# Opening the gate of the late output stores half a store earlier, in a batched matmul on one core

## The chip, the core and the metric

The kernel runs on one core of a Trainium2 chip. The metric is device microseconds of that core; the profile's span, from the first to the last instruction, is some 1.8 us shorter (515.2 beside 516.97 for the changed kernel). The executions of most kernels here lie within 0.3% of each other (six of the kernel before: 516.89 to 517.77 us), those of gate498, gate500, k8, pool8a and pool8b within 0.4 to 0.6%. All executions quoted here are marked as fast in their records. Every timed run was made in rounds with the kernel before on the same chip, and the ratio is formed from those rounds.

Names used below: TensorE (PE) does the matmuls, VectorE (DVE) and ScalarE (ACT) copy results out of PSUM (the memory that TensorE writes to), GpSimd (POOL) and SyncE (SP) issue DMAs. The data itself is moved by DMA engines, of which the profile counts 16. In the profile, q0 is the queue that POOL issues to, q1 the one that SP issues to, and q8 is of the kind "instruction": its packets follow the number of TensorE's instructions (20 for 5218, 15 for 3874, 8 for 2082, under A1 and mm5 below). The queues get in each other's way: from 495 to 500 us in the trace before, q1 takes 68.2% of the 16 engines' time, q0 24.8% and q8 1.2%, 94% in all, and in gate29, below, stores on q1 stretch the last loads of weights on q0 from 27.5 to 38.8 us (issue to landing).

## The reference

```python
x      = randn(32, 512, 1024)    # float32: batch, m, k
weight = randn(32, 1024, 768)    # float32: batch, k, n
out    = matmul(x, weight)       # float32: 32, 512, 768
```

## The kernel before

Loads go through q0, all but that of the first x, and are cast to bf16 on the way (the page: 167.77 MB read from HBM, but 126.88 MB moved on q0, of which 44.04 are the 28 stores). For each of 32 batches TensorE transposes x, multiplies, and the two copying engines empty PSUM into an output tile. A batch's output is one 1.5 MB tile: row tiles 0 and 1 are its first column half ("pair 0" below), row tiles 2 and 3 its second. The stores of batches 0 to 27 go through q0, between the loads. The stores of 28 to 31 are "late": they go through SP's queue.

SP issues the stores in the program's order, and it needs something to hold 28 and 29 back, whose data is ready long before (that of 29 at 477.64; in the trace before both go out behind the store of 30, the three within 3.20 us from 495.14). This is the gate: the store of 30, placed first. Its wait for the data of 30 (493.9 us from the start, below) delays everything behind it.

```python
    CHUNKED = {B - 4: (4, 4), B - 3: (4, 4), B - 2: (4, 4), B - 1: (4, 2, 2)}
    AHEAD = 3
    LATE = 4
    # ... pools, views ...
        for b in range(B):
            # ... load x of b + 4 and weights of b + 3, on gpsimd ...
            if 0 < b <= B - LATE:
                nc.gpsimd.dma_start(out=out_view[b - 1], in_=outs[b - 1])
            if b == B - 1:
                for late in (B - 2, *range(B - LATE, B - 2)):
                    nc.sync.dma_start(out_view[late], outs[late])
            outs[b] = out_pool.tile([P, MT * N], F32, name="out_sb")
            # ... batches that are not CHUNKED: two pairs of row tiles over all of k ...
            xT = {0: transpose(b, 0)}
            pms = [banks() for _ in range(2)]
            at = 0
            for n in CHUNKED[b]:
                last = at + n == KT
                for mt in range(MT):
                    if mt + 1 not in xT and mt + 1 < MT:
                        xT[mt + 1] = transpose(b, mt + 1)
                    matmuls(pms[mt // 2], mt % 2, xT[mt], b, range(at, at + n), True)
                    if last and mt % 2 == 1:
                        pair = mt // 2
                        evacuate(b, pair, pms[pair])
                        if b == B - 1:
                            cols = slice(pair * N2, (pair + 1) * N2)
                            nc.sync.dma_start(out_view[b, :, cols], outs[b][:, cols])
                at += n
```

## Time and profile before

| | before |
|---|---|
| median of 3 runs | 517.37 us (517.19 to 517.54) |
| span of the profiled execution | 515.6 us |
| TensorE busy | 83% |
| DMA engines busy | 8 to 9 tenths in every fortieth of the span but the last |
| gate opens, last half store issues | 495.14 us, 507.92 us |

The page of the kernel before. The first lines give each engine's busy time; in the two rows below them, each digit is the busy share of one fortieth of the span, in tenths:

```profile
span 515.6 us, 5976 instructions
PE 429.0 (83%) x2576; PEld 279.2 (54%) x2576; DVE 129.8 (25%) x196; ACT 76.3 (15%) x129; POOL 51.9 (10%) x102
...
PE   0999898698797888869978799797798877999793
...
DMA  8999999999999999999999999999999999999996
```

TensorE has holes all along, DMA has none. This is a kernel bound by DMA, and the question is only how its last 20 us end.

The timeline of the kernel before, ScalarE alone, and then SP alone (start, duration, engine, line, operation; what ended the idle time stands in brackets). A pair lies in three banks of PSUM; L111 and L113 copy the first and the third:

```profile
491.93 0.59 ACT L113 COPY out_sb<-pm 128x512 f32<-128x512 f32 x1 [0.78 <-PE pm L100]
493.12 0.59 ACT L111 COPY out_sb<-pm 128x512 f32<-128x512 f32 x1 [0.60 <-PE pm L100]
494.53 0.59 ACT L113 COPY out_sb<-pm 128x512 f32<-128x512 f32 x1 [0.82 <-PE pm L100]
...
507.31 0.59 ACT L113 COPY out_sb<-pm 128x512 f32<-128x512 f32 x1 [0.17 <-PE pm L100]
```

```profile
495.14 3.20 SPq L135 DMA_DIRECT2D out_dram<-out_sb  x3
506.62 1.63 SPq L164 DMA_DIRECT2D out_dram<-out_sb  x2
```

Batch 30's first pair is out of PSUM at 492.52 and its second at 495.12; the gate opens 0.02 us later. A gate on the first half would open 2.6 us earlier. The two half stores of 31 take 0.33 us each to issue, so the second of them starts at 506.62 + 1.63 - 0.33 = 507.92, right behind the last copy.

Is there idle DMA time that the earlier start could fill? The windows view (the stretch, its length, busy time of PE, PEld, DVE, ACT and POOL, granted clock, mean busy share of the DMA engines, GB/s):

```profile
494.00:495.00 1.00, 1.00 (x9) 0.96 (x8) 0.69 (x2) 0.47 (x1) 0.00 (x0) 1.00 0.73 283
495.00:496.00 1.00, 0.69 (x6) 0.39 (x6) 1.00 (x3) 0.11 (x1) 0.00 (x0) 1.00 0.70 289
```

There is: 0.27 + 0.30, about 0.57 us as a mean over 16 engines. A store of 128 rows leaves 16 landings in the trace, read here as one for each of the 16 DMA engines; the trace doesn't number them. These are the landings of the last half store of batch 31, from the trace's semaphore records (sorted; some 0.35 us behind the completion packets that the prediction quotes):

```
last half store of 31, before:   8th 511.73   12th 511.87   13th 513.17   16th 514.26
```

Twelve engines end together, four end 1.3 to 2.4 us after them, and the span ends behind the last.

### The profile page before, as it was taken

How to read it: one execution, taken by the hardware profiler on the slowest of the kernel's cores; microseconds unless marked ns; L12 is line 12 of the kernel's file. 1: busy time of each engine (PE TensorE's matmuls, PEld its weight loads, DVE VectorE, ACT ScalarE, POOL GpSimd, SP SyncE). 2: the span in 40 equal slices, each digit the busy share in tenths (PEclk: the TensorE clock that was granted, in tenths of full speed). 3: DMA queues.
4: the chain of work that ended last, by engine and by line, in shares of the span. 5: the costliest groups of instructions: out<-in, count | busy, mean ns of one | idle time of the engine just before them, and what ended most of it. 6: DMA issues, size and time to landing. Idle time of an engine off the chain costs nothing.

```text
span 515.6 us, 5976 instructions
## 1 busy us (share of the span) xinstructions
PE 429.0 (83%) x2576; PEld 279.2 (54%) x2576; DVE 129.8 (25%) x196; ACT 76.3 (15%) x129; POOL 51.9 (10%) x102
## 2 busy tenths in 40 slices
PE   0999898698797888869978799797798877999793
PEld 0666565465464555546645466464465545665461
DVE  0433232213232312221223232122222313232231
ACT  0011111111011111111111111011110111111011
POOL 3011100011011010100101001100111010111000
PEclk9999899989799988988989999799998989899898
DMA  8999999999999999999999999999999999999996
GB/s 255 218 218 211 218 271 275 256 237 276 277 275 269 231 273 276 274 274 245 251 278 276 274 260 242 272 274 275 269 243 263 277 273 275 247 248 272 274 368 285
DMA packets 14713, 135.64 MB, mean 263 GB/s; under 512 B 1632, under 2 KB 1632, under 8 KB 3040
## 3 DMA queue, kind: packets, MB, share of 16 engines
q0 software_dynamic: 13824, 126.88, 96.8%
q1 hardware_dynamic: 864, 8.39, 4.0%
q8 instruction: 20, 0.33, 0.2%
q14 instruction: 5, 0.04, 0.0%
HBM read 167.77 MB, written 50.33 MB: 423 GB/s over the span
## 4 chain that ended last, share of the span: by engine, by line
DMA 89%; PE 7%; issue 1%; POOL 1%; DVE 0%; ACT 0%; POOLq 0%
DMA w_sb<-in_weight_dram 39%; DMA x_sb<-in_x_dram 25%; DMA out_dram<-out_sb 25%; PE pm L100 7%; PE pt L69 1%; POOL w_sb L61 0%; POOL x_sb L55 0%; ACT out_sb L113 0%; DVE out_sb L112 0%; DVE xT L71 0%; POOL ident masks.py:199 0%; POOL ident masks.py:197 0%; POOLq L132 0%; POOLq L61 0%; POOLq masks.py:199 0%
## 5 line engine op out<-in xcount | busy, mean ns | idle before, releaser
L100 PE MATMUL pm<-w_sb,xT 128*128 128x256 bf16 (+1 forms) x2048 | 374.1, 342 | 66.1 <-DMA w_sb<-in_weight_dram 63.7
L100 PEld LDWEIGHTS <-xT 128*128 128x128 bf16 x2048 | 207.0, 102 | 208.2 <-issue 77.0
L71 DVE COPY xT<-pt 128x1024 bf16<-128x1024 bf16 x124 | 82.9, 689 | 230.6 <-PE pt L69 230.6
L111 ACT COPY out_sb<-pm 128x512 f32<-128x512 f32 x64 | 37.5, 587 | 293.3 <-PE pm L100 293.3
L69 PEld LDWEIGHTS pt<-ident,x_sb 128*128 128x128 f32 x496 | 72.7, 206 | 6.6 <-issue 1.9
L112 DVE COPY out_sb<-pm 128x512 f32<-128x512 f32 x64 | 44.0, 687 | 128.1 <-PE pm L100 128.1
L69 PE MATMUL pt<-ident,x_sb 128*128 128x128 f32 x496 | 75.3, 285 | 0.0
L113 ACT COPY out_sb<-pm 128x512 f32<-128x512 f32 x64 | 37.5, 587 | 137.5 <-PE pm L100 137.4
L55 POOL DMA_DIRECT2D x_sb<-in_x_dram x31 | 16.5, 534 | 176.5 <-DMA w_sb<-in_weight_dram 150.9
L61 POOL DMA_DIRECT2D w_sb<-in_weight_dram x37 | 19.8, 536 | 126.0 <-DMA out_dram<-out_sb 62.8
L132 POOL DMA_DIRECT2D out_dram<-out_sb x28 | 15.1, 538 | 119.0 <-DMA x_sb<-in_x_dram 57.3
L82 PE MATMUL pt<-ident,x_first 128*128 128x128 f32 x32 | 6.0, 350 | 12.2 <-DMA x_first<-in_x_dram 12.2
L82 PEld LDWEIGHTS pt<-ident,x_first 128*128 128x128 f32 x32 | 5.0, 204 | 12.8 <-issue 12.2
L83 DVE CAST xT<-pt 128x512 bf16<-128x512 f32 x8 | 5.6, 728 | 19.2 <-PE pt L82 19.0
L111 ACT ACT_TABLE_LOAD x1 | 1.3, 1283 | 0.7 <-PEq L180 0.7
masks.py:199 POOL TENSOR_SCALAR_AFFINE_SELECT ident<-ident 128x128 f32<-128x128 f32 x1 | 0.3, 289 | 0.1
masks.py:197 POOL MEMSET ident<- 128x128 f32 x1 | 0.2, 224 | 0.0
L180 POOL MEMSET const-float32-0.0<- 128x1 f32 x1 | 0.1, 99 | 0.2 <-issue 0.2
L180 POOL MEMSET const-bfloat16-1.0<- 128x1 bf16 x1 | 0.1, 102 | 0.0
L180 POOL MEMSET const-uint8-127<- 128x1 uint8 x1 | 0.1, 102 | 0.0
L180 POOL MEMSET const-float32-1.0<- 128x1 f32 x1 | 0.1, 99 | 0.0
## 6 DMA issues: line engine op xcount, KB each, us to landing
w_sb<-in_weight_dram POOLq DMA_DIRECT2D x28, 1536.0 KB, 43.2
out_dram<-out_sb POOLq DMA_DIRECT2D x28, 1536.0 KB, 42.0
x_sb<-in_x_dram POOLq DMA_DIRECT2D x31, 1024.0 KB, 39.6
w_sb<-in_weight_dram POOLq DMA_DIRECT2D x7, 768.0 KB, 31.4
out_dram<-out_sb SPq DMA_DIRECT2D x3, 1536.0 KB, 11.4
x_first<-in_x_dram SPq DMA_DIRECT2D x1, 2048.0 KB, 11.3
out_dram<-out_sb SPq DMA_DIRECT2D x2, 768.0 KB, 6.1
w_sb<-in_weight_dram POOLq DMA_DIRECT2D x2, 384.0 KB, 27.5
```

Of the source, the lines that this page charges most:

```text
L55: nc.gpsimd.dma_start(out=xs[b], in_=x_view[b])
L61: nc.gpsimd.dma_start(out=ws[b][:, at:at + n, :], in_=w_view[b, :, at:at + n, :])
L69: nc.tensor.transpose(pt[:, j, :], pairs[:, mt, j::JT], ident)
L71: nc.vector.tensor_copy(xT.rearrange("p j m r -> p (j m r)"), pt.bitcast(BF16).rearrange("p j m -> p (j m)"))
L82: nc.tensor.transpose(pt[:, i, :], x_first[:, mt, JT * h + i::KT], ident)
L83: nc.vector.tensor_copy(xT[:, 2 * h:2 * h + 2].rearrange("p j m r -> p j r m"), pt.rearrange("p (j r) m -> p j r m", r=2),)
L100: nc.tensor.matmul(pm[bank][:, at:at + size], xT[:, ko // 2, :, ko % 2], ws[b][:, ko, off:off + size], start=(ko == 0 and not (together an ...
L111: nc.scalar.copy(o[:, 0:512], pm[0])
L112: nc.vector.tensor_copy(o[:, 512:1024], pm[1])
L113: nc.scalar.copy(o[:, 1024:N2], pm[2])
L132: nc.gpsimd.dma_start(out=out_view[b - 1], in_=outs[b - 1])
L180: nc = _bacc.Bacc("TRN2", target_bir_lowering=False, num_devices=1)
```

## The change

The intent: let the late stores start as soon as half of batch 30 is evacuated, so that the DMA engines don't run dry between the last loads and the late stores. The second half of 30 goes behind 28 and 29, so that SP doesn't wait for it.

```diff
             if b == B - 1:
-                for late in (B - 2, *range(B - LATE, B - 2)):
+                halves = [slice(pair * N2, (pair + 1) * N2) for pair in range(2)]
+                nc.sync.dma_start(out_view[b - 1, :, halves[0]], outs[b - 1][:, halves[0]])
+                for late in range(B - LATE, B - 2):
                     nc.sync.dma_start(out_view[late], outs[late])
+                nc.sync.dma_start(out_view[b - 1, :, halves[1]], outs[b - 1][:, halves[1]])
@@
                         if b == B - 1:
-                            cols = slice(pair * N2, (pair + 1) * N2)
-                            nc.sync.dma_start(out_view[b, :, cols], outs[b][:, cols])
+                            nc.sync.dma_start(out_view[b, :, halves[pair]], outs[b][:, halves[pair]])
```

## The prediction

> **What bounds the kernel.** DMA. On the page, PE is busy 83% of the 515.6 us span, but the DMA row shows 8 or 9 tenths in every slice but the last, and the chain that ended last is 89% DMA. The change touches only the end.

> **The end before, from the timeline and the DMA packet records.** Batch 30's first column pair is evacuated by 492.53 us (last ACT copy at 491.93, 0.59 us), its second by 495.12. SP issues the whole store of 30 at 495.14, then 28 and 29; their first packets run at 495.98. PE has no DMA wait from 481.35 to 507.3. The half stores of batch 31 issue at 506.62 and 507.9; the last completion packet comes at 513.90 and the span ends 1.7 us later.

> The 16 DMA engines do not end together. Of the last store's 16 completions, 12 come at 511.26 to 511.52, three at 512.8 to 513.0, one at 513.90. The late ones were already behind in the gpsimd queue: the store of 27, last there, completes between 494.1 and 500.14. A packet of 12288 bytes takes 460 ns, and an engine has eight per whole store: 3.7 us. The last engine completes the store of 30 at 502.88, 28 at 506.54, 29 at 510.20, the halves of 31 at 512.05 and 513.90: steps of 3.66 and 1.85 us, without a gap. Back from 502.88, sixteen packets (stores 27 and 30) reach 495.5, where its last weight packet (495.33) ran. So this engine has no hole from before 492 to 513.90. The early engines have: in the windows 494:495 and 495:496 the DMA share drops to 0.73 and 0.70.

> **What the change does.** The gate opens at about 492.55 instead of 495.14; one 1.5 MB store becomes two of 0.75 MB, one more issue of about 0.35 us on an idle SP. Bytes are equal (6144-byte packets take 234 ns). No PE, ACT, DVE or gpsimd instruction moves.

> **What lies on the critical path.** Almost nothing. Starting earlier fills 0.5 to 0.6 us of mean DMA idleness at 494 to 496, on engines that finish 2.5 us early anyway. On the last engine the same packets are only reordered: [...] this trace agrees, with both queues' packets mixed from 496 to 499. So its end stays near 513.9. The price: the last weight chunk of batch 31 shares with stores and lands 2 to 3 us later (about 498 to 499 instead of 496). It is needed only in the last quarter of batch 31's matmuls, about 504.4 (11.5 us from 495.74 in parts 4:2:2), the chunk before at about 501.5. So PE should not wait.

> **Prediction.** 517.2 us (before 517.37), range 516.3 to 518.1. Faster by over 2%: 0.01, within 2%: 0.98, slower by over 2%: 0.01.

> **What would show it.** The SP issues in the timeline: first at about 492.6, the second half of 30 after 495.1. The share at 494 to 496 near 1. No weight wait of PE after 495, last ACT copy still at about 507.9. The last completion from one late engine within 0.7 us of 513.9.

> **What would make it wrong.** If the late engine loses time that its packet records hide, a second queue could fill it and end it up to 1 us earlier. If stores take more than half of the turns, the weight chunk could land after 501 to 504, PE would wait, and the end slip by 1 to 2 us. If the lag comes from the gpsimd queue and differs between executions, the tail moves by up to a microsecond.

## The result

| | before | after |
|---|---|---|
| median | 517.45 us, 6 runs | 517.21 us, 6 runs |
| range | 516.89 to 517.77 | 516.97 to 517.48 |
| ratio | | 0.9996, 95% interval 0.9983 to 1.0009 |
| span of the profiled execution | 515.6 us | 515.2 us |

A ratio here is the mean time of one kernel's fast runs over that of the other's of the same rounds, so it is not quite the ratio of the medians. A later run with five rounds ("again", below) gave 1.001 (0.9997 to 1.0024).

The change did what it was meant to do. SP's timeline after:

```profile
492.05 0.34 SPq L135 DMA_DIRECT2D out_dram<-out_sb  x1
492.45 1.37 SPq L137 DMA_DIRECT2D out_dram<-out_sb  x2
494.64 0.59 SPq L138 DMA_DIRECT2D out_dram<-out_sb  x1
506.12 1.63 SPq L166 DMA_DIRECT2D out_dram<-out_sb  x2
```

The gate opens 3.1 us earlier than in the trace before. Of that, 0.5 us is not the change: the whole profiled execution after ran 0.5 us earlier at this place already (the matching ScalarE copy, below, starts at 491.43 instead of 491.93, and TensorE's end is 0.5 us earlier too). The remaining 2.6 us are the change.

```profile
491.43 0.59 ACT L113 COPY out_sb<-pm 128x512 f32<-128x512 f32 x1 [0.78 <-PE pm L100]
```

SP's own waits (who waited for whom: us in total, times, longest) say the same, before and then after:

```profile
SPq L135 <- DVE out_sb L112: 493.9, 1, 493.9
```

```profile
SPq L135 <- DVE out_sb L112: 490.9, 1, 490.9
```

The idle DMA time is filled. The same windows after, with the stretch in which TensorE ends added:

```profile
494.00:495.00 1.00, 0.95 (x8) 0.76 (x7) 1.00 (x2) 0.58 (x1) 0.00 (x0) 1.00 0.95 363
495.00:496.00 1.00, 0.75 (x5) 0.49 (x6) 0.79 (x2) 0.00 (x0) 0.00 (x0) 1.00 1.14 479
505.00:508.00 3.00, 1.78 (x11) 0.87 (x9) 1.38 (x2) 2.09 (x4) 0.00 (x0) 1.00 0.78 326
```

In that last stretch the kernel before had:

```profile
505.00:508.00 3.00, 2.27 (x14) 1.18 (x12) 1.38 (x2) 2.30 (x4) 0.00 (x0) 1.00 0.94 395
```

So the gain is real and is given back. The share at 494 to 496 rises from 0.73 and 0.70 to 0.95 and 1.14 (the view counts a packet's whole time in the stretch in which it starts, so a share can pass 1), and at 505 to 508 it falls from 0.94 to 0.78. The engines that used to run dry before the late stores now run dry after them, while they wait for the last half stores of batch 31, which TensorE's last matmuls release. And the landings of the last half store:

```
         last issue    8th      12th     13th     16th landing
before   507.92        511.73   511.87   513.17   514.26
after    507.42        511.27   512.04   513.22   513.79
```

The last landing is 0.47 us earlier, which is the 0.5 us by which this execution ran ahead. Relative to the last issue, it comes 6.34 us later before and 6.37 us after. Nothing was gained. Nor has the last engine a pause: the last landings of SP's six late transfers after the change come at 500.95, 504.60, 508.25, 510.14, 511.96 and 513.79, in steps of 3.65 us for a store and 1.8 to 1.9 us for a half, which is what its packets take without a hole (eight of 460 ns, eight of 234 ns).

### The profile page after: what moved, and what is told of

Same layout as the page of the kernel before. It is cut to its first block, busy times and chain, and to the rows that moved or that the text cites. A ratio compares the mean times of both kernels' runs of the same rounds, so it can differ in the third digit from the quotient of the medians.

```text
span 515.2 us, 5979 instructions
## 1 busy us (share of the span) xinstructions
PE 429.3 (83%) x2576; PEld 279.5 (54%) x2576; DVE 129.8 (25%) x196; ACT 76.2 (15%) x129; POOL 51.7 (10%) x102
## 4 chain that ended last, share of the span: by engine, by line
DMA 88%; PE 8%; issue 1%; POOL 1%; DVE 0%; ACT 0%; POOLq 0%
DMA w_sb<-in_weight_dram 40%; DMA out_dram<-out_sb 25%; DMA x_sb<-in_x_dram 23%; PE pm L100 7%; PE pt L69 1%; POOL w_sb L61 0%; POOL x_sb L55 0%; DVE out_sb L112 0%; DVE xT L71 0%; ACT out_sb L113 0%; POOL ident masks.py:199 0%; POOL ident masks.py:197 0%; POOLq L132 0%; POOLq L61 0%; POOLq masks.py:199 0%
## 5 line engine op out<-in xcount | busy, mean ns | idle before, releaser
L55 POOL DMA_DIRECT2D x_sb<-in_x_dram x31 | 16.4, 532 | 176.8 <-DMA w_sb<-in_weight_dram 151.3
## 6 DMA issues: line engine op xcount, KB each, us to landing
w_sb<-in_weight_dram POOLq DMA_DIRECT2D x2, 384.0 KB, 27.5
```

The source lines that it names most:

```text
L55: nc.gpsimd.dma_start(out=xs[b], in_=x_view[b])
```

## The experiments

Theory A: the end is set by the most loaded DMA engine. It has work without a hole from before 492 us to its last packet, so an earlier start only changes the order of its packets. Its part A1, formed after reading the traces: what makes it the most loaded is the program. By A1 the 20 packets of 16384 bytes on q8 are fetches of TensorE's instructions, and they are not spread evenly over the engines.

The rivals are these: B, the end is the last issue plus a fixed time to land; C, the moment of the gate passes through to the end and the gain was hidden by noise; A2, four DMA engines are slow in themselves.

A1 came from this. The page lists the fetches of TensorE's program, the same in both kernels (a further queue, q14, brings five packets of 8192 bytes in either):

```profile
q8 instruction: 20, 0.33, 0.2%
```

```
fetch no. 1  at  32.0 us:  spread of the landings  0.62 -> 2.02
fetch no. 9  at 220.3 us:                          2.94 -> 4.02
fetch no. 17 at 424.4 us:                          3.99 -> 5.10
```

By this estimate, twenty fetches over eight engines are three each for four of them and two each for the other four. Four late engines are what the landings show. Not all of the spread is explained so: after its jump at fetch no. 1 it settles at 1.37 us, and it grows to 2.94 us before no. 9.

All of the following start from the changed kernel. Each was timed in three rounds (five for "again"), with a profile.

### drop28: one late store less (wrong result)

```diff
-                for late in range(B - LATE, B - 2):
+                for late in range(B - LATE + 1, B - 2):
```

> From the changed kernel, the store of batch 28 is left out on purpose (its output is wrong). Theory A (the span ends when the most loaded DMA engine has emptied its two queues without a hole; starting stores earlier only reorders its packets): that engine has 8 packets of 460 ns less, 3.7 us, so the end moves until the issue of the last half store limits it, about 511.3 on the scale of the trace after: 2.4 us earlier, about 514.8 us against 517.2. Rival B (the end is the last issue plus a fixed time for the last store to land): the same 517.2.

Measured: 514.41 us beside 516.98, ratio 0.9949 (0.9932 to 0.9966). The last half store lands on all 16 engines between 511.57 and 511.75, 3.84 us behind its issue at 507.91. With 3.7 us less to do, the late engines are no longer late, and the last issue is the limit. B falls: bytes that have nothing to do with the last issue moved the end. It also shows what tidying this tail could gain while the last issue stays where it is: about 2.5 us.

### mm5 and mm1: fewer TensorE instructions (wrong result)

The two lines of the batches 0 to 27 take fewer chunks of k; the DMA of data is unchanged.

```diff
-                            matmuls(pm, half, xT[half], b, range(KT), False)
+                            matmuls(pm, half, xT[half], b, (0, 1, 2, 3, KT - 1), False)   # mm5; mm1 has (0,)
@@
-                            matmuls(pm, half, xT[2 + half], b, range(KT), False)
+                            matmuls(pm, half, xT[2 + half], b, (0, 1, 2, 3, KT - 1), False)
@@
-                    stop=(ko == KT - 1),
+                    stop=(ko == KT - 1 or len(kos) == 1),                                 # mm1 alone
```

> From the changed kernel, batches 0 to 27 multiply 5 of the 8 k chunks (wrong result on purpose); all DMA of data is the same. The TensorE program falls from about 5218 to 3874 instructions. Theory A1 (the late DMA engines are late because they also fetch the program: 20 packets of 16384 bytes at about 0.93 us, dealt in turn to 8 of the 16 engines, so four engines have three of them): 15 packets, at most two on an engine, the last engine ends 0.93 us earlier, 516.3 us, and the last store's completions spread over about 1.8 us instead of 2.7. Rival A2 (four engines are slow in themselves, or slow on the gpsimd queue): no change, 517.2 us and a spread of 2.7.

> As mm5 but 1 of 8 k chunks in batches 0 to 27: about 2082 TensorE instructions. Theory A1: 8 fetch packets, one on each of 8 engines, the end 1.87 us earlier than the changed kernel, 515.3 us, spread about 0.9. Rival A2: no change, spread 2.7.

Measured: mm5 516.12 us, ratio 0.9982 (0.9967 to 0.9997); mm1 515.14 us, ratio 0.9966 (0.9951 to 0.9981); before 516.98 in the same rounds. That is 0.9 and 1.8 us less, as A1 had it. The fetches on the pages of mm5, then of mm1:

```profile
q8 instruction: 15, 0.25, 0.2%
```

```profile
q8 instruction: 8, 0.13, 0.1%
```

The expected spreads were a miss: the last half store's landings spread over 3.26 us in mm5 and 2.60 us in mm1, not 1.8 and 0.9. I had taken the 2.7 us of the changed kernel for the whole lag, but there the early engines wait for the last issue, which hides part of it. For the second half of 30, the transfer before the two halves of 31, nobody waits, and there the spread is 4.67 us in the changed kernel, 3.25 in mm5 and 2.59 in mm1 (other traces with 20 fetches, of "again" and drop28, have 4.52 and 5.07). So the fetches explain about 2.1 us of that lag; with one fetch on each of eight engines, by the estimate, some 1.7 us of lag (2.59 less one fetch of 0.93) remain, whose cause no run here shows. The trace of mm1 shows only when it arises: the landings of the gpsimd queue's transfers spread over 0.71 us at 73 us and over 2.45 us at 118 us, and between its fetches at 48.7 and 142.3 us there is none.

### mm1ld: the instructions back, without the matmuls (wrong result)

mm5 and mm1 also let TensorE finish earlier (last issue at 504.40 and 503.70). The control puts idle weight loads of one column into mm1:

```diff
             outs[b] = out_pool.tile([P, MT * N], F32, name="out_sb")
+            for _ in range(96):
+                nc.tensor.ldweights(ident.bitcast(BF16)[:, 0:1])
```

> Control for mm1: the same single k chunk in batches 0 to 27, plus 96 weight loads of one column per batch that feed no matmul: about 5154 TensorE instructions again, so 20 program fetches as in the changed kernel, but still only an eighth of the matmul work. Theory A1 (program fetches on the DMA engines make the last one late): back to 20 packets of 16384 bytes and to about 517.2 us. Rival (mm1 and mm5 were faster because TensorE was done earlier or released buffers earlier): stays at mm1's 515.1 us.

Measured: 517.88 us beside 517.48, ratio 1.0013 (0.9996 to 1.0029). TensorE's row of the page and the fetches:

```profile
PE 218.2 (42%) x1002; PEld 190.8 (37%) x4080; DVE 127.3 (25%) x196; ACT 76.2 (15%) x129; POOL 51.9 (10%) x102
...
q8 instruction: 20, 0.33, 0.2%
```

TensorE's matmul row is nearly as idle as in mm1 (42% busy beside 40%) and the time is back. The spread for the second half of 30 is 5.11 us again. One blemish: the 96 loads stand in batch 31 too and delay the last issue to 509.95, 2.5 us later than in the changed kernel. Fourteen engines therefore end at 513.81 or before, but the last still ends on its own work: it lands the second half of 30 at 510.68 and the halves of 31 at 512.58 and 514.38, in steps of 1.9 and 1.8 us, what a half store takes an engine without a pause. The spread, not the time alone, is what speaks for A1. A2 falls as the whole cause: 2.1 us of the lag come and go with the number of instructions. For the 1.7 us that stay it isn't excluded.

### gate498 and gate500: the gate later instead of earlier

The four stores move into the loop of batch 31, behind a one-column copy of VectorE inside the tile of batch 30, which VectorE reaches after the x transposes of row tile 2 (gate498) or 3 (gate500).

```diff
                     if mt + 1 not in xT and mt + 1 < MT:
                         xT[mt + 1] = transpose(b, mt + 1)
+                        if b == B - 1 and mt + 1 == 2:       # gate500: == 3
+                            edge = outs[b - 1][:, 0:1]
+                            nc.vector.tensor_copy(edge, edge)
+                            # ... the four stores of the changed kernel, moved here ...
```

> From the changed kernel, the gate is moved later: the four stores issue only after VectorE has copied the x transposes of row tile 2 of batch 31 (a one-column copy inside the tile of batch 30 behind them), about 498.5 on the scale of the trace before, 6 us later than changed and 3.4 later than before. Theory A: the last engine still has the store of 27 to work on until about 499.2 and loses nothing; the early engines start at 499.3, need 11.0 us for three stores and 3.7 for the halves of 31, and end near 514.1, so 517.2 to 517.8 us. Theory C (the time of the first late store's issue passes through to the end, and the change gained nothing only by chance): 3 to 6 us slower, 520 to 523.

> As gate498, but behind the transposes of row tile 3: the stores issue at about 500.3 on the scale of the trace before. By then every engine is empty from 499.2 on, so the whole backlog of 14.7 us moves with the gate: about 1.7 us slower than gate498 (518.5), 520 us, with all engines ending within 0.3 us of each other.

Measured: gate498 518.51 us (517.66 to 520.43), ratio 1.0034 (1.0013 to 1.0056); gate500 519.65 us (518.27 to 521.24), ratio 1.0059 (1.0040 to 1.0078). SP's timeline, gate498 and then gate500:

```profile
500.92 0.34 SPq L160 DMA_DIRECT2D out_dram<-out_sb  x1
```

```profile
498.74 0.34 SPq L160 DMA_DIRECT2D out_dram<-out_sb  x1
```

The profiled executions happen to stand in the wrong order: that of gate498 ran 2 us behind all through its end (it is the 520.43 us one), that of gate500 is its fastest. Taken by their own gates they agree: the last landing comes at 517.30 and 515.11, so 16.38 and 16.37 us behind the gate, and all 16 engines land within 0.21 us of each other. This is the plain time of the whole backlog when every engine starts it empty. It gives an estimate of the knee: before, 495.14 + 16.38 is 511.5, less than the 514.26 of the last engine; only a gate after about 514.26 - 16.38 = 497.9 should cost anything. By this estimate the kernel before already stood 2.8 us inside the free range, and the change moved it further in. No run has its gate between 495.14 and 498.74, so the knee itself isn't measured. C falls for the gates from 492.05 to 495.14 that were run: there the gate doesn't pass through. The expected 517.2 to 517.8 for gate498 was about 1 us too low; I had counted 0.85 us from the gate to the first packets and the bare packet times, and the measured 16.4 us is longer. Both kernels also scatter more (2.8 and 3.0 us) than the changed kernel (0.5 and 0.9 us), which fits: here the time of the gate, which follows TensorE, is no longer hidden. It is no proof, as k8 below scatters by 2.6 us.

### gate29: the gate much earlier

```diff
+            if b == B - 2:
+                for late in (B - 3, B - 4):
+                    nc.sync.dma_start(out_view[late], outs[late])
             if b == B - 1:
@@
-                for late in range(B - LATE, B - 2):
-                    nc.sync.dma_start(out_view[late], outs[late])
```

> The stores of 29 and 28 are issued when 29 is evacuated (about 477.7 on the scale of the trace before), 15 us earlier than in the changed kernel; the two halves of 30 as they come. Theory A: the bytes of the last engine are the same, so its end is moved only if TensorE is; two stores take up to 7.3 us of each engine's turns from the weight chunks of 30 and 31, which arrive 2 to 5 us later, TensorE shows a weight wait in batch 30 or 31, the last issue comes 2 to 5 us later than 507.9, and the time is 518 to 521 us. Rival (earlier stores are always as good or better): 517.2 us or less.

Measured: 521.90 us beside 517.48, ratio 1.0093 (1.0078 to 1.0108), slightly above the expected range; the last issue came 7.0 us later than 507.9, where 2 to 5 were expected. TensorE's waits for weights from 470 us on, in the changed kernel and then in gate29:

```profile
PE pm L100 <- DMA w_sb<-in_weight_dram: 3.4, 1, 3.4
```

```profile
PE pm L100 <- DMA w_sb<-in_weight_dram: 9.9, 2, 6.5
```

The one wait of the changed kernel is in batch 30; it has none after 482. Here the stores run beside the last weight chunks, whose time from issue to landing is 38.8 us instead of 27.5 (the two of 384 KB), TensorE waits 6.5 us more, and the last half store issues at 514.96 and lands 3.84 us later on all engines. So the gate is needed: at 477.34 the stores delay the weights of the last batches. Between that and the late limit lies a free range that holds at least the gates from 492.05 to 495.14; where it begins was not tested. The rival ("earlier is never worse") falls.

### order30: half of the change

```diff
                 nc.sync.dma_start(out_view[b - 1, :, halves[0]], outs[b - 1][:, halves[0]])
+                nc.sync.dma_start(out_view[b - 1, :, halves[1]], outs[b - 1][:, halves[1]])
                 for late in range(B - LATE, B - 2):
                     nc.sync.dma_start(out_view[late], outs[late])
-                nc.sync.dma_start(out_view[b - 1, :, halves[1]], outs[b - 1][:, halves[1]])
```

> The changed kernel, with the second half of 30 directly behind its first, so that 28 and 29 again wait until the whole of 30 is evacuated (about 495.1): only half a store goes out early. Theory A: the packets of the last engine are reordered once more: 517.2 us within 0.4. It also shows whether the order of the four stores matters at all.

Measured: 517.40 us beside 517.48, ratio 1.0002 (0.9987 to 1.0017). With the gate in its free range, this other order of the four stores makes no difference either.

### k8, pool8a and pool8b: attempts to unload the late engines

If the late engines can be given fewer bytes, the end should come up to 2.5 us earlier. k8 cuts the store of 28:

```diff
-                    nc.sync.dma_start(out_view[late], outs[late])
+                    if late == B - LATE:
+                        nc.sync.dma_start(out_view[late, 0:96], outs[late][0:96])
+                        for p in range(96, P, 8):
+                            nc.sync.dma_start(out_view[late, p:p + 8], outs[late][p:p + 8])
+                    else:
+                        nc.sync.dma_start(out_view[late], outs[late])
```

Which engines a store of 8 rows runs on wasn't known. The expectation reckons with eight of the 16, which then carry two packets more than before, and the other eight two less. D1 stands for late engines that are all among the other eight, D2 for late engines of which some or all are among those of the 8-row stores.

> The changed kernel, with the store of 28 cut in a DMA of 96 rows (six rows on each of 16 engines) and four of 8 rows. [...] Theory D1[...]: the last one is relieved of two packets, 0.92 us, and the time is about 516.3 us. Theory D2[...]: 0.92 us later, about 518.1 us.

Measured: 519.02 us (518.29 to 520.90) beside 517.48, ratio 1.0040 (1.0016 to 1.0063). The direction is D2's; the size is larger than 0.9 us and scatters. The four small issues keep SP busy for 8.28 us (1.19 to 2.65 us each, where an issue on an empty queue took 0.33 us):

```profile
493.28 8.28 SPq L140 DMA_DIRECT2D out_dram<-out_sb  x4
```

Each 8-row store leaves nine semaphore records instead of 16, one soon after the issue and eight from landings, which are read here as those of eight engines. These landings, beside those of the 96-row store that stands before them in the same queue, tell whether late engines are among the eight:

```
96 rows, last seven:     502.56  502.90  503.40  503.56  503.73  504.08  505.29
first 8 rows, last three:     503.02  503.36  504.21
last landings of the four 8-row stores:  504.21  504.66  505.14  505.67
```

If each engine works through a queue in order, an 8-row store lands a packet (0.46 us) behind the 96 rows on the same engine. 503.02, 503.36 and 504.21 fit 502.56, 502.90 and 503.73, and nothing follows 504.08 and 505.29. So the two latest engines of this trace are not among the eight, but the late engine of 503.73 is: with its extra packets it lands at 505.67, behind the 505.29 of the formerly latest, and it ends last. So there are late engines among the eight and outside them, which D2 allowed, and this cut takes packets from some of them and gives them to another. That part of the extra 1.5 us which isn't bytes was not separated.

pool8a and pool8b try the same with the store of 27 on gpsimd. Which engines its small transfers would run on was the author's guess, not shown by any trace: the expectations reckon with all the bulks of pool8a on one half of the engines, called upper if it is the half without the late engines and lower if it is the half with them, and with those of pool8b on the other half. Without such a split, both were expected near 517.2 us, or slower by the extra issues:

```diff
-                nc.gpsimd.dma_start(out=out_view[b - 1], in_=outs[b - 1])
+                if b < B - LATE:
+                    nc.gpsimd.dma_start(out=out_view[b - 1], in_=outs[b - 1])
+                else:
+                    nc.gpsimd.dma_start(out=out_view[b - 1, 0:96], in_=outs[b - 1][0:96])
+                    for p in range(96, P, 8):
+                        for cols in (slice(0, 128), slice(128, MT * N)):   # pool8b: the other way round
+                            nc.gpsimd.dma_start(out=out_view[b - 1, p:p + 8, cols], in_=outs[b - 1][p:p + 8, cols])
```

> An attempt at a faster version: in the changed kernel, the store of 27 on the gpsimd queue is cut into 96 rows (six on each engine) and four times 8 rows, each of these as a sliver of 128 columns and then the bulk. [...] If that is the upper half, the late engines[...] lose two packets each: 0.9 us faster, 516.3 us. If it is the lower half: 0.9 us slower, 518.1. [...]

> As pool8a with bulk first and sliver second[...]: the opposite sign of pool8a by theory A (the last engine's bytes decide): one of the two 516.3 us, the other 518.1. [...]

Measured: pool8a 517.68 us (516.56 to 518.68), ratio 1.0010 (0.9992 to 1.0028); pool8b 517.21 us (516.86 to 519.03), ratio 1.0008 (0.9989 to 1.0028); before 517.21 us. No opposite signs and no gain: a failed attempt. The eight extra gpsimd DMAs also waited for earlier transfers (1.3 to 5.8 us each) and were issued one by one up to about 503 us, so these runs don't tell whether the bulks all fell on one half. The expectation also took the late engines to be all in one half; by the landings of k8 they lie on both sides of the split there, so it isn't shown that either run could have spared them all. A version that beats both kernels was not found.

### again: the changed kernel, five rounds

> The changed kernel itself once more, to narrow the interval of its ratio to the kernel before. Theory A (the last engine's bytes and program fetches set the end): a ratio of 0.999 to 1.001, no gain outside noise, with the last completion of the last store from an engine that worked without a hole. Theory C (0.2 to 0.5 us of the 2.6 us earlier issue pass through to the end): 0.9990 to 0.9995 with an interval that excludes 1.

Measured: 517.46 us (517.22 to 518.12) beside 517.01, ratio 1.0010 (0.9997 to 1.0024). With the first comparison (0.9996), the two kernels are the same; C's gain of 0.2 to 0.5 us is not there. The trace of this run is also the best evidence for the last engine. Its gate opens at 493.58 and its last half store issues at 508.95, 1.5 us later than in the first trace of the changed kernel, but the last landing, at 514.18, is only 0.4 us later. What stays the same is the time from the last landing of the last weight chunk to the very last landing: 18.35 us before (495.91 to 514.26), 18.38 after (495.41 to 513.79) and 18.39 here (495.79 to 514.18), with three different gates. That is the packet time of the five stores 27 to 31 on one engine: five times the 3.66 us that the prediction read from the trace before is 18.3 us.

## Why the prediction was right

- **The time:** 517.2 us was predicted and 517.21 measured, within 2%. The agreement to 0.01 us is luck, as the runs of one kernel scatter by 0.5 to 0.9 us. The mechanism held: the same bytes on an engine without a hole, so an earlier start is worth nothing. drop28 shows that the backlog of the late engines sets the end, the three spans of 18.35 to 18.39 us under "again" that this backlog doesn't feel the gate, and gate498 with gate500 that a gate at 498.74 or later does count.
- **The gate:** predicted at about 492.55; 492.05 in a trace that ran 0.5 us ahead. Right.
- **The idle DMA time:** predicted to be filled, on engines that don't matter. Right; the profile after shows it reappear at 505 to 508.
- **TensorE:** predicted not to wait for weights after 495. Right: after 482 its only wait in the profile is 0.3 us for VectorE.
- **"Lands 2 to 3 us later":** wrong, without effect on the time. The last weight chunk of 31 landed at 495.91 before and at 495.41 after, so at the same time once the 0.5 us are taken off. I had let SP's packets take every second turn from the moment of issue, an estimate that no trace had shown. In fact the first ones ran at 494.12, 2.07 us after the issue, when the last weight packets (494.83) were nearly through; before, with some engines already empty, the first packets ran 0.84 us after the issue. So the two queues began to share the engines later than estimated. Why was not tested, but other traces show a pattern: the first packets ran 0.84 us after the issue in before, again, gate498 and gate500, where some engines had by then finished the gpsimd queue, and 3.4 to 3.5 us after it in mm5, mm1 and gate29, where none had. In the trace after, 494.12 is also when the first engine finished that queue's last store. So the packets of both queues that the prediction saw mixed from 496 to 499 ran for the most part on different engines: from 497 to 498, when four engines still had gpsimd packets, these kept 3.5 to 4.0 engines busy; only from 498.5 on, with one such engine left, did they take about half of it (0.54).
- **"If the lag comes from the gpsimd queue":** the prediction left the cause of the late engines open and suspected the queue. The runs show another: mm5, mm1 and mm1ld tie about 2.1 us of it to the fetches of TensorE's program. The rest of the lag, some 1.7 us, stays open.

## What to carry to other kernels

When DMA is the limit, ask for each DMA engine, not for their mean, whether it has a hole: the landings of one large transfer, sorted, show in one line how many engines finish late, and idle time on the others was worth nothing here (0.57 us of it filled, ratio 0.9996). In these runs the end of the kernel is the latest of three times (last issue plus 3.84 us, gate plus 16.4 us, and the most loaded engine's work), and moving one that isn't the latest changes nothing; a test that takes bytes away finds the one that counts. A program of thousands of TensorE instructions is DMA traffic too: here 5218 of them came with 20 packets of 0.89 to 1.0 us, and with 8 packets the time was 1.8 us less (mm1), more than this schedule change had to win.
